# w2 of FFN 1 in five groups: T2 by accumulating transfers, low parts by VectorE, and a new order around the first norms

## The chip, the cores and the metric

The kernel runs on one core of one Trainium2 chip. The metric is the device time of one execution in microseconds (us). Before the change the median of three runs is 1115.6 us (1115.53 to 1117.86).

The engines are named as the profile names them: PE (TensorE) does matrix products, PEld is its weight load, DVE (VectorE) and ACT (ScalarE) work element by element, POOL (GpSimd) and SP (SyncE) here mostly issue transfers. Each engine works through its own list of instructions in order; semaphores hold an instruction until what it needs is there.

## The reference

One layer of a streaming encoder on a batch of one, 512 tokens, width 1024, all in float32:

```python
h = x + 0.5 * post1(SwiGLU_1(pre1(x)))          # D_FF = 2816
u = pre_mix(h)
q, k, v, x_rnn, x_gate = split(u @ w_in)
yA = griffin(x_rnn, x_gate)                      # conv(4), RG-LRU scan, gelu gate
yB = window_attention(q, k, v)
h = h + post_mix((gateA * yA + gateB * yB) @ w_o)
y = h + 0.5 * post2(SwiGLU_2(pre2(h)))
def swiglu(x, w1, w3, w2):
    return (jax.nn.silu(x @ w1) * (x @ w3)) @ w2
```

`pre`, `post` and `pre_mix` are RMS norms with a gain. The change is in the product of the first SwiGLU with its w2 (2816 by 1024), in the norm behind it (post1, then pre_mix), and in the first weights of w_in (the blocks called xr, for x_rnn) which are made ready meanwhile.

## The kernel before

**Three products for one.** TensorE multiplies in a shortened float format (fp32r). To keep float32 accuracy each operand is split into a high part and a low part, and each product is made as hi times hi, plus lo times hi, plus hi times lo. The high part is a copy by ScalarE into the short format (`whi`, L651 for w2, L159/L178 for other weights; `uT`, `hx`, `hT` by L213 for the hidden activations). The low part, `wlo`, comes in one of two ways. Either VectorE subtracts high part from raw value (L659, L179; L214 for activations). Or "by add": ScalarE writes the negated copy (L653, L656, L160), and a transfer issued by POOL adds the raw values onto it while it writes (L654, L657, L161).

**w2 of FFN 1.** The 22 blocks of 128 rows of w2 are worked in two ways. Twenty of them form five groups (`GS_A`, G = 5) of four blocks, each taken as a 2 by 2 block product with seven instead of eight multiplications (class `Halves`, with the Winograd form of Strassen's scheme). The seven are named m1, m5, m2, m6, m3, m7, m4 and are run in that order, five groups each: 35 units, numbered u = 0 to 34, of 12 matmuls with 512 columns (L680 to L682). The weights of a group are b11, b12, b21 and b22. The scheme needs T1 = b12 - b11 for m5 and T2 = b22 - T1 for m2 and for later differences, and similar sums of the activations (`S`, L590). T1 is made by add: ScalarE writes -b11 (L601) and a transfer adds b12 (L602). T2 is a VectorE subtraction (`t2`, L587), for groups 0 to 2 in the units of m5, for 3 and 4 in those of m2. b22 is loaded by SP (L580), and once more for m3 (L665), since it was overwritten.

The remaining two blocks, the tail (`TAIL_A` = 2, 3), are multiplied in the plain way (`classical`, L242 to L244). Their hidden activations are the `kept` blocks (L1318 to L1325).

**Preparing and multiplying.** `step(u)` first prepares unit u + LEAD, LEAD being 5 (`prep`: high part, low part, split of the activations, then the sums), runs hooks that are attached to u, and then issues the unit's matmuls. Bank results are copied out behind the last unit of an m (`out`: L694 on ScalarE, L692 on VectorE for m7). Which units' low parts are made by add stands in the code: m2 of groups 0 to 3, the set `ADD_A` (m6 and m7 of groups 3 and 4, m4 of group 1), and the tail by `BY_DMA`.

**The order around the norms** is written out in `tok_gemm`, in its branch for `pre`: units 0 to 24, the tail products of token tiles 0 and 1, preparation up to unit 31, norm(0); the five units of m7, tail products of tiles 2 and 3, the rest of the preparations, norm(1); then for tiles 2 and 3 in turn half of m4's matmuls, the transposes (L341) of tile t - 2, their copies into `uT` (L351 on ScalarE, L353 on VectorE), and the remaining tail products; norm(2) falls in the first turn. Then the next weights (xr) are split, and norm(3) and the xr products (L224 to L226) follow. A norm starts on VectorE with L294, or L297, and ends with `hg` (L331 on VectorE, L332 on ScalarE), which the transposes need.

**Buffers.** All large tiles share one pool of 42 slots (`NSLOT`). A slot is free again when the last reader of its tile is done; the next tile in program order then takes it. So ScalarE, which writes most new tiles first, can be held by TensorE, which reads the old ones last.

## Time and profile before

| | us |
|---|---|
| median of three runs | 1115.6 |
| profiled execution, its own time | 1117.63 |
| its span | 1115.8 |
| PE busy (98%) | 1097.1 |
| DVE busy (84%) | 934.5 |
| ACT busy (63%) | 698.2 |
| POOL busy (36%) | 404.0 |
| w2 of FFN 1 on PE, first unit to first product of xr | 232.24 to 352.02 |

The mean granted clock of TensorE is 0.993 of full speed. The profiled execution was 2.0 us longer than the median; 1.8 us of its time lie outside the span.

How to read it: busy shares are means over stages with different limits. In the stage of w2 of FFN 1 (about 232 to 352 us) the engines hand work on in a ring: ScalarE and VectorE (or a transfer) make a unit's operands ready, TensorE uses them and frees their slots, and ScalarE needs a free slot for the next one. So the rows to look at are what each engine waited for, and at which time. A row of the timeline has a start, a duration, the engine, the line, the operation, output <- inputs with their shapes; in brackets stand the idle time before it and what ended that.

### The profile page before, as it was taken

What the parts mean: (1) busy time and instruction counts of PE and PEld (TensorE: products, weight loads), DVE (VectorE), ACT (ScalarE), POOL (GpSimd) and SP (SyncE); (2) the same over time, 40 slices, a digit from 0 to 9 for tenths busy, and PEclk for the clock granted to TensorE, in tenths of its full rate; (3) what the DMA queues carried; (4) which work ended last, traced back from release to release, by engine and by line L of the source; (5) the groups of instructions that cost most, each with busy time, mean ns of one, the idle gap of its engine ahead of it and who ended that gap; (6) DMA issues with size and microseconds to landing.
All of it is one profiled execution on the core that took longest, in us unless ns stands there. A gap on an engine that the chain in (4) does not pass through costs nothing.

```text
span 1115.8 us, 18010 instructions
## 1 busy us (share of the span) xinstructions
PE 1097.1 (98%) x6826; PEld 988.5 (89%) x6826; DVE 934.5 (84%) x1329; ACT 698.2 (63%) x1207; POOL 404.0 (36%) x337
## 2 busy tenths in 40 slices
PE   9999999999888999999999999999999999999997
PEld 7899999987677877899888888888999999998886
DVE  5978999999868978878677875867789989999995
ACT  7756555587876677856565665346555555467672
POOL 0144833222111523043555564010777566521000
PEclk9999999999989999999999999999999999999999
DMA  9325653498784572126322345251433233647642
GB/s 333 122 89 131 151 124 114 133 245 196 196 206 135 162 177 99 57 83 247 126 85 87 95 170 208 79 224 58 142 104 114 84 106 96 206 136 186 189 115 92
DMA packets 53926, 159.07 MB, mean 143 GB/s; under 512 B 5568, under 2 KB 7488, under 8 KB 53840
## 3 DMA queue, kind: packets, MB, share of 16 engines
q1 hardware_dynamic: 44640, 132.19, 34.6%
q0 software_dynamic: 8912, 25.21, 11.9%
q8 instruction: 53, 0.87, 0.3%
q10 hardware_dynamic: 288, 0.52, 0.2%
q14 instruction: 33, 0.27, 0.1%
HBM read 137.47 MB, written 13.62 MB: 135 GB/s over the span
## 4 chain that ended last, share of the span: by engine, by line
PE 88%; ACT 4%; issue 3%; DMA 3%; DVE 2%; POOL 0%; DVEq 0%; SPq 0%; POOLq 0%; ACTq 0%
PE c L798 13%; PE c L800 13%; PE c L799 13%; PE f L224 9%; PE f L225 9%; PE f L226 9%; PE hw L681 4%; PE hw L680 3%; PE hw L682 3%; PE acc L242 1%; PE acc L244 1%; PE acc L243 1%; DMA wlo<-raw_w2a 1%; PE pt L1652 1%; DMA wlo<-in_w2a_dram 1%
## 5 line engine op out<-in xcount | busy, mean ns | idle before, releaser
L799 PE MATMUL c<-uT,wlo 128*128 128x256 f32 x516 | 146.0, 283 | 0.0
L800 PE MATMUL c<-uT,whi 128*128 128x256 f32 x516 | 146.0, 283 | 0.0
L798 PE MATMUL c<-uT,whi 128*128 128x256 f32 x516 | 146.0, 283 | 0.0
L798 PE MATMUL c<-Xh,whi 128*128 128x256 f32 x504 | 142.7, 283 | 0.0
L799 PE MATMUL c<-Xh,wlo 128*128 128x256 f32 x504 | 142.6, 283 | 0.0
L224 PE MATMUL f<-uT,whi 128*128 128x512 f32 (+1 forms) x368 | 137.2, 373 | 0.0
L226 PE MATMUL f<-uT,whi 128*128 128x512 f32 (+1 forms) x368 | 135.4, 368 | 0.2 <-DVE uT L353 0.2
L225 PE MATMUL f<-uT,wlo 128*128 128x512 f32 (+1 forms) x368 | 135.3, 368 | 0.0
L800 PE MATMUL c<-Xl,whi 128*128 128x256 f32 x456 | 129.1, 283 | 0.0
L214 DVE TENSOR_TENSOR wlo<-S,whi 128x1024 fp32r<-128x1024 f32 x86 | 121.0, 1407 | 7.3 <-POOL OL L1688 4.5
L213 ACT ACTIVATE whi<-S 128x1024 fp32r<-128x1024 f32 x86 | 88.5, 1055 | 30.2 <-DVE S L847 28.0
L799 PEld LDWEIGHTS c<-uT,wlo 128*128 128x128 f32 x516 | 99.0, 192 | 0.2
L798 PEld LDWEIGHTS c<-uT,whi 128*128 128x128 f32 x516 | 99.0, 192 | 0.2
L800 PEld LDWEIGHTS c<-uT,whi 128*128 128x128 f32 x516 | 99.0, 192 | 0.0
L798 PEld LDWEIGHTS c<-Xh,whi 128*128 128x128 f32 x504 | 96.8, 192 | 0.3 <-issue 0.3
L799 PEld LDWEIGHTS c<-Xh,wlo 128*128 128x128 f32 x504 | 96.8, 192 | 0.0
L681 PE MATMUL hw<-wlo,uT 128*128 128x512 f32 x228 | 89.3, 392 | 1.7 <-DMA wlo<-raw_w2a 1.0
L682 PE MATMUL hw<-whi,uT 128*128 128x512 f32 x228 | 88.9, 390 | 0.0
L680 PE MATMUL hw<-whi,uT 128*128 128x512 f32 x228 | 88.8, 389 | 0.0
L800 PEld LDWEIGHTS c<-Xl,whi 128*128 128x128 f32 x456 | 87.5, 192 | 0.0
L224 PEld LDWEIGHTS f<-uT,whi 128*128 128x128 f32 x368 | 70.1, 190 | 12.9 <-issue 1.7
L226 PEld LDWEIGHTS f<-uT,whi 128*128 128x128 f32 x368 | 69.9, 190 | 11.8 <-DVE uT L353 0.4
(439 smaller groups left out, 3184.5 us busy)
## 6 DMA issues: line engine op xcount, KB each, us to landing
raw_w2b<-in_w2b_dram SPq DMA_DIRECT2D x27, 512.0 KB, 4.5
raw_w2a<-in_w2a_dram SPq DMA_DIRECT2D x22, 512.0 KB, 7.3
raw_w1b<-in_w1b_dram SPq DMA_DIRECT2D x22, 512.0 KB, 4.3
raw_w3b<-in_w3b_dram SPq DMA_DIRECT2D x22, 512.0 KB, 4.4
raw_w3a<-in_w3a_dram SPq DMA_DIRECT2D x21, 512.0 KB, 4.7
raw_w1a<-in_w1a_dram SPq DMA_DIRECT2D x20, 512.0 KB, 4.6
raw_wg<-in_wg_dram SPq DMA_DIRECT2D x16, 512.0 KB, 3.7
h<-in_x_dram SPq DMA_DIRECT2D x8, 512.0 KB, 6.3
```

The costliest lines, as they stand in the source:

```text
L213: act.activation(hi, src, AF.Copy)
L214: dve.tensor_tensor(out=lo, in0=src, in1=f32(hi), op=ALU.subtract)
L224: pe.matmul(ps[:, c0:c1], wh[:, s], h_, start=k == 0 and c0 == 0, stop=False, skip_group_check=True)
L225: pe.matmul(ps[:, c0:c1], wl[:, s], h_, start=False, stop=False, skip_group_check=True)
L226: pe.matmul(ps[:, c0:c1], wh[:, s], l_, start=False, stop=k == KT - 1, skip_group_check=True)
L242: pe.matmul(acc[n], x[:, 0, c], wh[:, s], start=first, stop=False, skip_group_check=skip)
L680: pe.matmul(ps, xs[:, 0, j, c], hi[:, j, :], start=start and j == 0, stop=False, skip_group_check=True)
L681: pe.matmul(ps, xs[:, 0, j, c], lo[:, j, :], start=False, stop=False, skip_group_check=True)
L682: pe.matmul(ps, xs[:, 1, j, c], hi[:, j, :], start=False, stop=i == self.G - 1, skip_group_check=True)
L798: pe.matmul(ps, wh[:, s], xh, start=first, stop=False, skip_group_check=True)
L799: pe.matmul(ps, wl[:, s], xh, start=False, stop=False, skip_group_check=True)
L800: pe.matmul(ps, wh[:, s], xl, start=False, stop=k == 3, skip_group_check=True)
```

## The change

It has four parts.

1. `add_t` takes the place of `add_t1`: for FFN 1, T2 too is made by add, for all five groups. ScalarE writes -T1 into a new slot (the same helper, `T_load`, as for T1), and a transfer issued by POOL adds b22 from HBM. This stands in the units of m5. VectorE's five subtractions for T2 are gone, and so are SP's five first loads of b22.
2. All low parts of w2 of FFN 1 that were made by add are now VectorE subtractions: four of m2, two of m6, two of m7, one of m4, two of the tail; eleven in all. ScalarE's negated copies and POOL's transfers for them are gone.
3. The preparations of m4 of groups 0 and 1 move from ahead of norm(0) to behind it (5G + LEAD + 2 becomes 5G + LEAD). The two gain vectors are loaded five units later, and the scaling of one of them by ScalarE moves from unit 20 to just ahead of norm(0).
4. The splits of the weight blocks xr2 and xr3 move from just ahead of norm(3) to m4's units 31 and 33, which in program order is behind norm(1) and ahead of norm(2).

In total ScalarE has 6 instructions fewer in its list (1038 to 1032), VectorE 6 more (1289 to 1295), POOL 6 fewer (277 to 271), SP 5 fewer (268 to 263). TensorE's order is the same.

ScalarE in the units of m5; `whi` is the high part of T1, `uT<-hEO` a high part of activations. Before:

```order
L651 ACTIVATE whi_2914<-raw_w2a_2739 128x1024
L213 ACTIVATE uT<-hEO_788 128x512
L651 ACTIVATE whi_2936<-raw_w2a_2763 128x1024
L213 ACTIVATE uT<-hEO_1316 128x512
L651 ACTIVATE whi_2958<-raw_w2a_2793 128x1024
```

After:

```order
L659 ACTIVATE whi_2904<-raw_w2a_2739 128x1024
L213 ACTIVATE uT<-hEO_788 128x512
L596 ACTIVATE raw_w2a_2910<-raw_w2a_2739 128x1024
L659 ACTIVATE whi_2928<-raw_w2a_2763 128x1024
L213 ACTIVATE uT<-hEO_1316 128x512
L596 ACTIVATE raw_w2a_2934<-raw_w2a_2763 128x1024
```

Behind each unit's pair now stands a third copy, the negated T1 (L596), onto which the transfer adds b22.

VectorE from the middle of m3's and m7's preparations to the start of norm(0), which is the L294 row; `hT` are the tail's activations. Before:

```order
L214 TENSOR_TENSOR hT_3366<-kept_440,hT_3366 128x512
L659 TENSOR_TENSOR wlo_3387<-raw_w2a_2599,whi_3386 128x1024
L214 TENSOR_TENSOR uT<-hEO_1316,uT 128x512
L214 TENSOR_TENSOR hT_3392<-kept_535,hT_3392 128x512
L659 TENSOR_TENSOR wlo_3415<-raw_w2a_2601,whi_3414 128x1024
L214 TENSOR_TENSOR uT<-hEO_1837,uT 128x512
L214 TENSOR_TENSOR uT<-hEO_2338,uT 128x512
L214 TENSOR_TENSOR uT<-hEO_482,uT 128x512
L659 TENSOR_TENSOR wlo_3487<-raw_w2a_2934,whi_3486 128x1024
L214 TENSOR_TENSOR hx_3488<-hEO_789,hx_3488 128x512
L214 TENSOR_TENSOR hx_3495<-hEO_1317,hx_3495 128x512
L294 TENSOR_TENSOR hc_2999<-hw_3128,hc_2999 128x512
```

After:

```order
L179 TENSOR_TENSOR wlo_3363<-raw_w2a_499_3274,whi_3362 128x1024
L667 TENSOR_TENSOR wlo_3379<-raw_w2a_2599,whi_3378 128x1024
L214 TENSOR_TENSOR uT<-hEO_1316,uT 128x512
L214 TENSOR_TENSOR hT_3384<-kept_535,hT_3384 128x512
L179 TENSOR_TENSOR wlo_3388<-raw_w2a_502_3295,whi_3387 128x1024
L667 TENSOR_TENSOR wlo_3406<-raw_w2a_2601,whi_3405 128x1024
L214 TENSOR_TENSOR uT<-hEO_1837,uT 128x512
L667 TENSOR_TENSOR wlo_3424<-raw_w2a_2717,whi_3423 128x1024
L214 TENSOR_TENSOR uT<-hEO_2338,uT 128x512
L667 TENSOR_TENSOR wlo_3470<-raw_w2a_2719,whi_3469 128x1024
L214 TENSOR_TENSOR uT<-hEO_482,uT 128x512
L294 TENSOR_TENSOR hc_2998<-hw_3120,hc_2998 128x512
```

Four low parts are new ahead of the norm (two L179 of the tail, and `wlo_3424` and `wlo_3470` of m7), and the first units of m4 (`wlo_3487` with the two `hx`) are gone from there.

VectorE from the end of norm(1), whose last row is L331, to the start of norm(2). Before:

```order
L331 SCALAR_TENSOR_TENSOR hg_3656<-h_3400,r_586_3686,bc_mix_pre_g_3126 128x512
L353 TENSOR_TENSOR uT<-tr_3726,uT 128x4x128
L353 TENSOR_TENSOR uT<-tr_3731,uT 128x4x128
L294 TENSOR_TENSOR hc_3112<-acc_3635,hc_3112 128x512
L297 SCALAR_TENSOR_TENSOR fg_3752<-hc_3112,bc_ffn_post_g_3124 128x512
```

After:

```order
L331 SCALAR_TENSOR_TENSOR hg_3645<-h_3391,r_586_3675,bc_mix_pre_g_3231 128x512
L179 TENSOR_TENSOR wlo_3698<-raw_xr_557_3580,whi_3697 128x1024
L179 TENSOR_TENSOR wlo_3714<-raw_xr_564_3608,whi_3713 128x1024
L353 TENSOR_TENSOR uT<-tr_3723,uT 128x4x128
L353 TENSOR_TENSOR uT<-tr_3728,uT 128x4x128
L294 TENSOR_TENSOR hc_3109<-acc_3624,hc_3109 128x512
L297 SCALAR_TENSOR_TENSOR fg_3749<-hc_3109,bc_ffn_post_g_3229 128x512
```

The low parts of xr2 and xr3 (L179) now stand between norm(1) and the copies of the first transposed tile. Where they stood before, from the end of norm(2) to norm(3). Before:

```order
L331 SCALAR_TENSOR_TENSOR hg_3748<-h_3565,r_604_3777,bc_mix_pre_g_3126 128x512
L353 TENSOR_TENSOR uT<-tr_3817,uT 128x4x128
L353 TENSOR_TENSOR uT<-tr_3822,uT 128x4x128
L179 TENSOR_TENSOR wlo_3838<-raw_xr_557_3591,whi_3837 128x1024
L179 TENSOR_TENSOR wlo_3842<-raw_xr_564_3619,whi_3841 128x1024
L294 TENSOR_TENSOR hc_3112<-acc_3642,hc_3112 128x512
```

After:

```order
L331 SCALAR_TENSOR_TENSOR hg_3745<-h_3554,r_608_3774,bc_mix_pre_g_3231 128x512
L353 TENSOR_TENSOR uT<-tr_3814,uT 128x4x128
L353 TENSOR_TENSOR uT<-tr_3819,uT 128x4x128
L294 TENSOR_TENSOR hc_3109<-acc_3631,hc_3109 128x512
L297 SCALAR_TENSOR_TENSOR fg_3877<-hc_3109,bc_ffn_post_g_3229 128x512
```

Norm(3) now follows the transposed tile directly.

The diff:

```diff
@@ -419,8 +419,7 @@
 
         if pre:
             G = pre.G
-            pre.hooks[2 * G].append(vectors)
-            pre.hooks[4 * G].append(lambda: act.activation(g[1], g[1], AF.Copy, scale=NEWT))
+            pre.hooks[3 * G].append(vectors)
             for i in range(2):
                 pre.hooks[6 * G - 2 + i].append(lambda i=i: [split_to(st["get"] + i + 1), dma_to(st["get"] + i + 3)])
             for u in range(5 * G):
@@ -430,7 +429,8 @@
                 acc[t] = [pre.bank["bc"][t], pre.bank["bx"][t]]
                 for n_ in range(2):
                     classical(t, n_)
-            pre.prep(5 * G + LEAD + 2)
+            pre.prep(5 * G + LEAD)
+            act.activation(g[1], g[1], AF.Copy, scale=NEWT)
             norm(0)
             for u in range(5 * G, 6 * G):
                 pre.step(u)
@@ -438,10 +438,13 @@
                 acc[t] = [pre.bank["bu"][t - 2], bank("acc")]
                 classical(t, 1)
             pre.prep(7 * G)
+            pre.hid.eo.clear()
             norm(1)
             for t in range(2, 4):
                 for u in range(6 * G, 7 * G):
                     pre.step(u, (t - 2,))
+                    if t == 2 and u % G % 2:
+                        split_to(st["split"] + 1)
                 trs[t - 2] = transpose_mm(us[t - 2])
                 transpose_out(trs[t - 2], t - 2, xf if t == 2 else None)
                 classical(t, 0)
@@ -449,7 +452,6 @@
                     norm(2)
             split_to(st["get"] + len(first))
             dma_to(st["split"] + 2)
-            pre.hid.eo.clear()
             pre.bank.clear()
         else:
             tails()
@@ -555,14 +557,14 @@
 
         names = ("m1", "m5", "m2", "m6", "m3", "m7", "m4")
 
-        def __init__(self, nm, hid, hooks, gs, by_add, in_slots, add_t1):
+        def __init__(self, nm, hid, hooks, gs, by_add, in_slots, add_t):
             self.nm, self.hid, self.hooks, self.gs = nm, hid, hooks, gs
             self.by_add, self.in_slots = by_add, in_slots
             self.G = G = len(gs)
-            self.loads = [(b, i) for i in range(G) for b in (("b11",) if add_t1 else ("b11", "b12"))]
+            self.loads = [(b, i) for i in range(G) for b in (("b11",) if add_t else ("b11", "b12"))]
             self.first = len(self.loads)
-            self.loads += [(b, i) for b in ("b22", "b21") for i in range(G)]
-            self.add_t1 = add_t1
+            self.loads += [(b, i) for b in (("b21",) if add_t else ("b22", "b21")) for i in range(G)]
+            self.add_t = add_t
             self.again_at = self.names.index("m3") * G - 3
             self.raw, self.ops, self.loaded, self.ready = {}, {}, 0, 0
             self.bank, self.c, self.again, self.did = {}, {}, {}, set()
@@ -589,17 +591,23 @@
         def S(self, o, p, q, i, op=ALU.subtract):
             dve.tensor_tensor(out=self.x(i, *o), in0=self.x(i, *p), in1=self.x(i, *q), op=op)
 
+        def T_load(self, o, q, i):
+            t = self.raw[o, i] = slot([P, 2, 512], name=f"raw_{self.nm}")
+            act.activation(t, self.raw[q, i], AF.Copy, scale=-1.0)
+            pool.dma_start(out=t, in_=self.src(o, i), accum_op=ALU.add)
+
         def t2(self, i):
-            self.T("b22", "b22", "b12", i)
+            if self.add_t:
+                self.T_load("b22", "b12", i)
+            else:
+                self.T("b22", "b22", "b12", i)
             del self.raw["b12", i]
 
         def t1(self, i):
             if ("t", i) not in self.did:
                 self.did.add(("t", i))
-                if self.add_t1:
-                    t = self.raw["b12", i] = slot([P, 2, 512], name=f"raw_{self.nm}")
-                    act.activation(t, self.raw["b11", i], AF.Copy, scale=-1.0)
-                    pool.dma_start(out=t, in_=self.src("b12", i), accum_op=ALU.add)
+                if self.add_t:
+                    self.T_load("b12", "b11", i)
                 else:
                     self.T("b12", "b12", "b11", i)
 
@@ -614,11 +622,11 @@
                 self.t1(i)
                 self.s1(i)
             elif m == "m5":
-                if i < T2_EARLY:
+                if i < T2_EARLY or self.add_t:
                     self.t2(i)
                 self.S((0, 0), (0, 1), (0, 0), i)
             elif m == "m2":
-                if i >= T2_EARLY:
+                if i >= T2_EARLY and not self.add_t:
                     self.t2(i)
                 self.T("b11", "b22", "b11", i)
                 self.S((1, 0), (1, 0), (0, 0), i)
@@ -639,7 +647,7 @@
                 self.ready += 1
                 m, i = self.names[u // G], u % G
                 if load:
-                    self.load(min(self.first + 2 * G, self.first + (u if u >= U_SLOTS else u == 3)))
+                    self.load(self.first + (max(0, u - G) if self.add_t else u if u >= U_SLOTS else u == 3))
                 b, odd, half = self.OPERANDS[m]
                 hi = slot([P, 2, 512], F32R, name="whi")
                 lo = slot([P, 2, 512], F32R, name="wlo")
@@ -649,7 +657,7 @@
                     xs = uT[:, :, (u + 1) % 8, :].rearrange("p e (j c) -> p e j c", j=2)
                 src = self.again.pop(i) if m == "m3" else self.raw[b, i]
                 act.activation(hi, src, AF.Copy)
-                if m == "m2" and i < 4:
+                if m == "m2" and i < 4 and not self.add_t:
                     act.activation(lo, src, AF.Copy, scale=-1.0)
                     pool.dma_start(out=lo, in_=self.src(b, i), accum_op=ALU.add)
                 elif (m, i) in self.by_add:
@@ -708,7 +716,7 @@
                 later(0, lambda: self.out(m), 0)
             point()
 
-    def blocks(nm, hid, pairs, late, h_src, gs, marks, by_add, in_slots, loads, add_t1=False):
+    def blocks(nm, hid, pairs, late, h_src, gs, marks, by_add, in_slots, loads, add_t=False):
 
         hooks = {u: [] for u in range(7 * len(gs))}
 
@@ -723,7 +731,7 @@
         for at_, fn in zip(marks, (lambda n: dma_to(st["get"] + n + 1), tail_tile, h_back)):
             for n, u in enumerate(at_):
                 hooks[u].append(lambda n=n, fn=fn: fn(n))
-        half = Halves(nm, hid, hooks, gs, by_add, in_slots, add_t1)
+        half = Halves(nm, hid, hooks, gs, by_add, in_slots, add_t)
         pairs.more = lambda n: half.load(loads[n])
         ahead = lambda: half.prep(min(half.ready + 1, U_SLOTS))
         end = len(pairs.jobs) - 1
@@ -1808,7 +1816,7 @@
 GRAW_AT = (29, 30)
 TB_AT = (34, 35, 36, 37)
 
-BY_DMA = {("wg", i) for i in range(2)} | {("w2a", i) for i in (2, 3)} | {("xr", i) for i in range(2)}
+BY_DMA = {("wg", i) for i in range(2)} | {("xr", i) for i in range(2)}
 
 BY_POOL = {("wg", i) for i in range(2, 8)} | {("wk", 0), ("wk", 1)}
 
@@ -1819,7 +1827,7 @@
 LOAD_A, LOAD_B = (0, 3, 5, 5), (0, 6, 8, 10)
 GS_A = (4, 6), (8, 10), (12, 14), (16, 18), (0, 20)
 MARKS_A = (17, 18), (21, 22), (20, 22, 27, 29)
-ADD_A = {(m, i) for m in ("m6", "m7") for i in (3, 4)} | {("m4", 1)}
+ADD_A = set()
 
 TAIL_B = (20, 21)
 GS_B = (0, 2), (4, 6), (8, 10), (12, 14), (16, 18)
```

## The prediction

> **What bounds the kernel now.** I read first how busy the engines are over the whole span, then the busy time by stretches around w2 of FFN 1, then TensorE's waits there, and last VectorE's own rows.
>
> ```profile
> PE 1097.1 (98%) x6826; PEld 988.5 (89%) x6826; DVE 934.5 (84%) x1329; ACT 698.2 (63%) x1207; POOL 404.0 (36%) x337
> ```
>
> ```profile
> 364.25:1100.00 735.75, 735.75 (x4512) 660.16 (x4511) 616.32 (x881) 450.08 (x805) 302.46 (x235) 1.00 0.41 132
> 232.24:295.85 63.61, 61.87 (x270) 49.75 (x269) 63.51 (x80) 48.21 (x65) 10.11 (x10) 1.00 0.90 240
> 309.12:315.95 6.83, 5.98 (x14) 4.73 (x15) 3.11 (x4) 4.02 (x6) 1.51 (x2) 0.50 0.99 232
> 363.72:367.14 3.42, 3.42 (x18) 3.42 (x17) 1.95 (x3) 3.11 (x7) 0.36 (x1) 0.50 1.00 382
> ```
>
> The columns are the stretch, its length, then busy time of PE, PEld, DVE, ACT, POOL, then granted clock, DMA share and GB/s. From 364.25 to 1100 TensorE is never idle and the change touches nothing there, so what it gains or loses by 364 reaches the end one for one. In the w2 stage VectorE is full instead (63.51 of 63.61 us), and TensorE runs into waits:
>
> ```profile
> PE hw L243 <- DMA wlo<-in_w2a_dram: 5.3, 2, 4.0
> PE tr L341 <- DVE hg L331: 3.4, 1, 3.4
> PE hw L681 <- DMA wlo<-raw_w2a: 1.0, 1, 1.0
> PE hw L681 <- DMA wlo<-in_w2a_dram: 0.8, 3, 0.3
> ```
>
> Columns: total, times, longest. The tail blocks' low parts by DMA cost 5.3 us and, behind the 4.0 us wait, the clock of 0.50 for 6.83 us, in which 5.98 us of busy time do the work of 3.0. Yet that is not what sets the end. TensorE waits once more, 3.4 us for `hg` of the fourth norm, norm(3), and that is the end of a VectorE chain:
>
> ```profile
> 239.19 1.22 DVE L659 TENSOR_TENSOR wlo<-raw_w2a,whi 128x1024 fp32r<-128x1024 f32 x1
> 240.32 0.68 DVE L214 TENSOR_TENSOR uT<-hEO,uT 128x512 fp32r<-128x512 f32 x1
> 240.93 1.21 DVE L587 TENSOR_TENSOR raw_w2a<-raw_w2a,raw_w2a 128x1024 f32<-128x1024 f32 x1
> 254.90 1.21 DVE L587 TENSOR_TENSOR raw_w2a<-raw_w2a,raw_w2a 128x1024 f32<-128x1024 f32 x1
> 284.75 0.68 DVE L1318 TENSOR_TENSOR kept<-kept,Rb 128x512 f32<-128x512 f32 x1
> 315.97 0.68 DVE L294 TENSOR_TENSOR hc<-hw,hc 128x512 f32<-128x512 f32 x1
> 324.32 0.75 DVE L331 SCALAR_TENSOR_TENSOR hg<-h,r,bc_mix_pre_g 128x512 f32<-128x512 f32 x1
> 326.09 1.23 DVE L659 TENSOR_TENSOR wlo<-raw_w2a,whi 128x1024 fp32r<-128x1024 f32 x1 [1.01 <-ACT whi L651]
> 334.57 0.68 DVE L294 TENSOR_TENSOR hc<-hw,hc 128x512 f32<-128x512 f32 x1
> 341.69 0.75 DVE L331 SCALAR_TENSOR_TENSOR hg<-h,r,bc_mix_pre_g 128x512 f32<-128x512 f32 x1
> 342.94 1.29 DVE L353 TENSOR_TENSOR uT<-tr,uT 128x512 fp32r<-128x512 f32 x2 [0.49 <-ACT uT L351]
> 344.14 0.68 DVE L294 TENSOR_TENSOR hc<-acc,hc 128x512 f32<-128x512 f32 x1
> 352.00 1.29 DVE L353 TENSOR_TENSOR uT<-tr,uT 128x512 fp32r<-128x512 f32 x2 [0.49 <-ACT uT L351]
> 353.44 1.23 DVE L179 TENSOR_TENSOR wlo<-raw_xr,whi 128x1024 fp32r<-128x1024 f32 x1
> 355.71 0.68 DVE L294 TENSOR_TENSOR hc<-acc,hc 128x512 f32<-128x512 f32 x1
> ```
>
> Columns: start, duration, engine, line. L294 starts a norm (315.97, 334.57, 344.14, 355.71). Start to start, a 1024-wide subtraction takes 1.13 us (239.19 to 240.32) and a 512-wide one 0.61 (240.32 to 240.93). I use these pitches, not the longer durations, because neighbours overlap.
>
> TensorE's own rows at the end of the stage:
>
> ```profile
> 352.02 0.39 PE L224 MATMUL f<-uT,whi 128*128 128x256 f32 x1
> 359.35 0.28 PE L225 MATMUL f<-uT,wlo 128*128 128x256 f32 x1
> 359.47 0.28 PE L226 MATMUL f<-uT,whi 128*128 128x256 f32 x1
> 363.14 1.45 PE L341 MATMUL tr<-ident,hg 128*128 128x128 f32 x8 [3.39 <-DVE hg L331]
> ```
>
> The first xr products start at 352.02, as soon as the second token tile is transposed, and are over at about 359.6.
>
> **The change, along VectorE's chain.**
>
> *To the end of m6.* Five T2 subtractions (L587) go, four low parts of m2 and two of m6 come: 6 - 5 = +1 times 1.13 = +1.1 us. For T2 ScalarE now writes a negated copy, and its rows give the price:
>
> ```profile
> 236.83 1.04 ACT L601 ACTIVATE raw_w2a<-raw_w2a 128x1024 f32<-128x1024 f32 x1
> 237.78 1.04 ACT L651 ACTIVATE whi<-raw_w2a 128x1024 fp32r<-128x1024 f32 x1
> 238.73 0.62 ACT L213 ACTIVATE uT<-hEO 128x512 fp32r<-128x512 f32 x1
> 239.25 1.05 ACT L651 ACTIVATE whi<-raw_w2a 128x1024 fp32r<-128x1024 f32 x1
> ```
>
> A wide copy takes 0.95 us, a narrow one 0.52. A unit of m5 costs ScalarE 0.95 + 0.95 + 0.52 = 2.42 us and VectorE 1.13 + 2 x 0.61 = 2.35, so for five units ScalarE is the slower by 0.4; two evacuations of m1 (L692) add up to 1.0 on ScalarE. VectorE thus waits 0 to 1.4 us; I take 1.1. m6 ends at 284.75 + 1.1 + 1.1 = 287.0.
>
> T2's transfer itself, bounded from both sides:
>
> ```profile
> raw_w2a<-in_w2a_dram POOLq DMA_DIRECT2D x5, 512.0 KB, 9.4
> DMA to landing us min/median/max: 3.6/7.3/13.9
> ```
>
> The same kind (T1) takes 9.4 us in the middle; the shortest raw transfer of w2 3.6, the longest 13.9. T2 of group 0 starts when ScalarE has written its copy, at about 240.2 in m5. VectorE first reads it in m2, at 254.90 now, less three T2 subtractions, plus one low part: 252.6, plus up to 1.4 of waits. So 3.6 and 9.4 cost nothing and 13.9 up to 1.5 us; I take nothing, by T1's row, and the later groups have more time, since a unit of m2 is longer than one of m5.
>
> Eleven other accumulating transfers and five plain loads go from a stretch with DMA at 0.90, so later transfers should not get slower; the loads of b21 on SP stay at their units. POOL loses six instructions and its two broadcasts move five units later, far ahead of the norm that reads them. The scaling of the gain, one wide copy on ScalarE, moves to just ahead of the first norm: 0 if ScalarE is idle there, 0.95 if not. I take 0, since VectorE is the later one there, with its two tail low parts.
>
> *From m6 to the first norm.* VectorE does four narrow instructions for the kept blocks (L1318 and its like), ten units of m3 and m7 with 1.13 + 0.61 each, two narrow for the tail's hidden blocks and two wide low parts for the tail: 2.4 + 17.4 + 1.2 + 2.3 = 23.3 us. The two m4 units are now behind the norm. In the trace this stretch holds long waits:
>
> ```profile
> DVE hx L214 <- ACT hx L213: 3.4, 1, 3.4
> DVE wlo L659 <- ACT whi L651: 3.1, 3, 2.2
> DVE uT L214 <- ACT uT L213: 3.1, 2, 1.9
> ```
>
> That is 9.6 us between 295 and 316, and I let all of it go: ScalarE was held by TensorE, which held the weight slots while it waited for the tail's DMA, and that wait ends with the DMA. The tail's second low part is now ready at about 305, 1.7 us after TensorE wants it, in place of 5.3. The first norm starts at 287.0 + 23.3 = 310.3, 5.7 us ahead of 315.97. TensorE's tail products are done by about 309.7, in time.
>
> *First to second norm.* The norm holds VectorE for 9.0 us (315.97 to about 325.0): 319.3. Then come all five m4 units, 5 x 1.74 = 8.7, two evacuations of m7 (1.2), and waits of the kind seen at 326.09 (1.01 for ScalarE, which also splits two xr blocks there): 2.6 in sum, from one such wait for each of two or three units. The second norm starts at 331.85 against 334.57: half the lead is spent on m4.
>
> *Second to third norm.* `hg` comes 7.12 us after the norm's start (334.57 to 341.69), at 339.0. New here: low parts of xr2 and xr3, 2.3 us, and about 1.1 us of waiting for ScalarE's high parts. With the transposed tile behind it the third norm starts at 344.2, against 344.14: the lead is gone.
>
> *Third to fourth norm.* Now it comes back: the xr low parts that stood at 353.44 are already done, so the fourth norm starts when the uT rows at 352.00 end, at 353.3 and not at 355.71. Its transposes can start 363.14 - 355.71 = 7.43 later, at 360.7 against 363.14: a gain of 2.4 us.
>
> *TensorE beside it.* Of 10.1 us (5.3 + 1.0 + 0.8 of waits and 3.0 of half clock) it gets back 1.7 at the tail and, by my sums of VectorE's lateness, 0.5 each in m6 and m4, and comes to the end of the m4 products at 352.0 - 10.1 + 2.7 = 344.6. There it has nothing: the xr products need the tile of 352.00. It idles 7.4 us, which is new. The trace shows what such a gap does: 0.50 of the clock from 309.12 after the 4.0 us, and from 363.72 after 3.39 us, both lifted in steps of 3.42 us. From 352.0 there are about 50 matmuls at 0.12 us (359.35 to 359.47) and 0.9 for a transposition, 7.0 us at full clock. Half clock for one to two steps (3.4 to 6.8 us) loses 1.7 to 3.4: ready between 360.7 and 362.4; on the steps of this trace (363.72 less two is 356.9, where it lifts), 361.45. It takes VectorE's place as the last by 0.75 us. Behind it there is no more idle time, so the 0.50 from 363.72 to 367.14, which loses 1.7, goes too.
>
> The Trainium skill ("TensorE: Matmul & The Clock Gate", section "Part 1: The HAM clock gate (the "warmup" mystery)") says that the clock is halved after an idle window of about 3.4 us and that the windows run free of the kernel. That speaks against this change, which makes the longest gap of the stage; the trace agrees (0.50 after 4.0 and 3.39 us idle), and a window that falls badly gives the later of the two ends above.
>
> **The sum** against the profiled run, 1117.63 us with a span of 1115.8: 361.45 - 363.14 = -1.7, and -1.7 for the clock: -3.4, so 1114.2. The median is 1115.6, 2.0 us below that run. Such a run may well lack the 1.7 of the second half clock, since a gap of 3.39 us hardly fills a step of 3.42; against it the gain would be 1.7 and the time 1113.9. If the 2.0 us are something else, 3.4 and 1112.2. Nothing shown tells which, so I take the middle, 2.5: **1113.1 us**.
>
> **The rivals.**
> *More gain.* The waits that I added (1.1 + 2.6 + 1.1 = 4.8 us) stay away. Then the tile of 352.0 comes at 347.2, TensorE's gap is 2.7 us, too short for the half clock, and it is ready at 354.2; the norm sets 355.9. Gain 7.2: 1108.4; with half of the waits about 1110.5. For it: ScalarE has 15 us free in the 63.6. Against: each of the waits has a row like it.
>
> *No difference.* Of the 9.6 us that I remove, 2 to 5 stay, since a unit of m3 asks for ScalarE and VectorE in turn. Each us delays all three later norms; 0.75 is free, the rest counts: 1113.1 + 2 - 0.75 = 1114.3 up to 1117.4.
>
> *Slower.* The ring of three closes in m3 and m7:
>
> ```profile
> L651 ACT ACTIVATE whi<-raw_w2a 128x1024 fp32r<-128x1024 f32 x26 | 27.3, 1052 | 12.9 <-PE hw L681 6.3 <-DMA raw_w2a<-in_w2a_dram 4.4 <-PE hw L682 2.2
> ```
>
> Between 239 and 316 ScalarE's high parts waited 8.5 us for slots that TensorE held. If TensorE, late in m6 and m3 because VectorE now makes every low part, holds them again, VectorE keeps waits as before. My margin is about 3 us of TensorE's lateness. With all 9.6 us the first norm starts at 319.9, 4 us after 315.97, and the end is at 1113.1 + 9.6 - 0.75 = 1122.0. It crosses the bound with 5.5 us.
>
> *The change doesn't do what it says* has no room: the new order on every engine shows each step.
>
> **The numbers.** 0.2% is 2.2 us, about what a measurement can tell: faster means below 1113.4, slower above 1117.8. The forecast has 0.42, its own range 1111.5 to 1114.2, 0.30 of it below 1113.4; more gain 0.18; no difference 0.18; slower 0.22. So faster 0.48, same 0.30, slower 0.22. The range goes from 1109.5 (most of the waits absent) to 1118.5 (6.2 of the 9.6 us kept).
>
> **What would show it.** Right: no wait of TensorE for a DMA of w2; norms starting near 310, 332, 344 and 353; a new gap of TensorE near 344 to 352 with half clock behind it; no gap at the fourth norm's transposes. Wrong: VectorE waiting for ScalarE by more than 3 us before the first norm; TensorE waiting for T2's DMA in m2; the third norm after 346, which hands every further us to the end; or the gap at 352 closed, which would mean that the chain is shorter than I summed.

## The result, and the profile after

The changed kernel takes 1114.18 us (median of 14 runs, 1113.33 to 1115.43). In the same comparison the kernel before takes 1117.26 us (median of 14 runs, 1115.53 to 1120.01). The ratio is 0.9973, with a 95% interval of 0.9965 to 0.9981: 3.1 us, or 0.27%, faster. The profiled execution of the changed kernel took 1113.81 us with a span of 1112.0, against 1117.63 and 1115.8 before.

Note the kernel before: its median was 1115.6 over the three runs that the prediction saw, and is 1117.26 over fourteen. Its profiled execution was close to the middle, and the median of three was at the low end.

The profile page of the changed kernel, engines' busy time:

```profile
PE 1094.1 (98%) x6826; PEld 986.9 (89%) x6826; DVE 940.6 (85%) x1335; ACT 692.1 (62%) x1201; POOL 398.6 (36%) x331
```

VectorE has 6.1 us more to do than before, and the kernel is faster. So the gain cannot be read from the busy shares; it is in the waits. TensorE's waits from 232 to 365 us (total, times, longest):

```profile
PE f L224 <- ACT uT L351: 4.4, 1, 4.4
PE hw L688 <- DVE hc L700: 2.9, 1, 2.9
PE hw L243 <- DVE wlo L179: 1.3, 1, 1.3
PE hw L689 <- DVE wlo L667: 0.7, 1, 0.7
```

No wait for a DMA is left. The 5.3 us for the tail's transfers have become 1.3 us for VectorE's low part, and the 3.4 us ahead of the fourth norm's transposes are gone. Two waits are new: 2.9 us at the start of m4, and 4.4 us for the second transposed tile. VectorE's waits from 295 to 316, where there were 9.6 us before:

```profile
DVE e L263 <- ACT r L259: 1.4, 1, 1.4
```

That one lies within norm(0), and the kernel before has it too. VectorE's timeline, at the places the prediction named (L1326 is the end of m6, L294 starts a norm, L331 ends one):

```profile
286.86 0.68 DVE L1326 TENSOR_TENSOR kept<-kept,Rb 128x512 f32<-128x512 f32 x1
310.12 0.69 DVE L294 TENSOR_TENSOR hc<-hw,hc 128x512 f32<-128x512 f32 x1
331.63 0.68 DVE L294 TENSOR_TENSOR hc<-hw,hc 128x512 f32<-128x512 f32 x1
340.47 2.36 DVE L179 TENSOR_TENSOR wlo<-raw_xr,whi 128x1024 fp32r<-128x1024 f32 x2 [0.95 <-ACT whi L178]
343.95 0.68 DVE L294 TENSOR_TENSOR hc<-acc,hc 128x512 f32<-128x512 f32 x1
353.08 0.68 DVE L294 TENSOR_TENSOR hc<-acc,hc 128x512 f32<-128x512 f32 x1
359.70 0.75 DVE L331 SCALAR_TENSOR_TENSOR hg<-h,r,bc_mix_pre_g 128x512 f32<-128x512 f32 x1
```

And TensorE's timeline, its idle times at m4's start and at the second tile, and its transposes of the fourth norm, which follow a product without a gap:

```profile
329.10 0.47 PE L688 MATMUL hw<-whi,hx 128*128 128x512 f32 x1 [2.90 <-DVE hc L700]
351.89 0.58 PE L224 MATMUL f<-uT,whi 128*128 128x256 f32 x1 [4.42 <-ACT uT L351]
360.47 0.28 PE L226 MATMUL f<-uT,whi 128*128 128x256 f32 x1
360.59 0.60 PE L341 MATMUL tr<-ident,hg 128*128 128x128 f32 x4
```

The clock by stretches (columns as in the prediction):

```profile
351.90:355.47 3.57, 3.57 (x17) 3.35 (x18) 3.11 (x6) 2.07 (x7) 0.00 (x0) 0.55 0.68 243
355.47:360.59 5.12, 5.12 (x45) 5.12 (x44) 4.63 (x13) 3.99 (x10) 0.00 (x0) 1.00 0.41 126
364.00:1100.00 736.00, 736.00 (x4509) 659.70 (x4508) 617.15 (x884) 448.77 (x803) 301.82 (x235) 1.00 0.41 130
```

After the gap of 4.42 us the clock is half until about 355.1, one step of 3.41 us (the first row holds a little of full clock too, so its mean is 0.55). Since TensorE had time there, this costs nothing that VectorE does not cost anyway. From 364 on TensorE is full, as before. The fourth transposes come 363.14 - 360.59 = 2.55 us earlier, and the half clock from 363.72 to 367.14, which lost 1.7, is gone: 4.25 us in sum. TensorE's last matmul starts 4.18 us earlier (1104.62 instead of 1108.80). The span fell by 3.8, since in these two executions the time behind the last matmul was some 0.4 us longer after the change.

### The profile page after: what moved, and what is told of

Read it like the earlier page. It is cut to its first block, busy times and chain, and to the rows that moved or that the text cites. A ratio compares the mean times of both kernels' runs of the same rounds, so it can differ in the third digit from the quotient of the medians.

```text
span 1112.0 us, 17985 instructions
## 1 busy us (share of the span) xinstructions
PE 1094.1 (98%) x6826; PEld 986.9 (89%) x6826; DVE 940.6 (85%) x1335; ACT 692.1 (62%) x1201; POOL 398.6 (36%) x331
## 4 chain that ended last, share of the span: by engine, by line
PE 94%; DVE 2%; ACT 2%; issue 1%; DMA 0%; DVEq 0%; SPq 0%; ACTq 0%
PE c L806 13%; PE c L807 13%; PE c L808 13%; PE f L224 10%; PE f L226 9%; PE f L225 9%; PE hw L690 5%; PE hw L688 5%; PE hw L689 5%; PE acc L243 1%; PE acc L242 1%; PE acc L244 1%; PE pt L1660 1%; DVE wlo L667 1%; PE s L1624 1%
```

## The experiments

The theory: from m5 to the fourth norm one chain of VectorE's work, with what it waits for, sets the time at which the fourth norm's transposes can start; TensorE behind it is always full. Every instruction taken from VectorE, and every wait, counts as long as TensorE or ScalarE is not later. The main rival: the gain is simply TensorE's 5.3 us of waiting for the tail's transfers with the half clock behind it. All ratios are to the kernel before, run on the same chip.

### Undoing part 4: the splits of xr2 and xr3

```diff
                     pre.step(u, (t - 2,))
-                    if t == 2 and u % G % 2:
-                        split_to(st["split"] + 1)
```

> The changed kernel with part 4 undone: the splits of xr2 and xr3 stand again just ahead of norm(3). Theory (VectorE's chain through the four norms sets the time): norm(2) starts 3.3 us earlier (2.3 of low parts and 1.0 of waiting gone from ahead of it), at 340.6 instead of 343.95; the transposed tile is ready at 348.5 instead of 351.9, so TensorE's gap of 4.4 us at 347.5 shrinks to about 1; norm(3) then starts behind the two low parts at 352.0 instead of 353.1, its transposes at 359.5 instead of 360.6, and TensorE waits for them some 4 us, with half clock behind that costing 1.7. In sum -1.1 + 1.7: 1114.8 us, within 1 of the changed kernel's 1114.2. Rival (part 4 alone is what brings the gain at the fourth norm, as my sum had it: 2.3 us come back): 1116.5.

Measured: 1114.5 us (1113.2 to 1114.91), ratio 0.9977 (0.9969 to 0.9986). TensorE's wait, the stretch behind it (clock third from the end), and VectorE's start of norm(3):

```profile
359.91 1.97 PE L341 MATMUL tr<-ident,hg 128*128 128x128 f32 x8 [3.39 <-DVE hg L331]
359.90:367.00 7.10, 7.09 (x49) 7.10 (x50) 4.09 (x5) 6.09 (x10) 2.86 (x2) 0.79 1.00 381
352.48 0.68 DVE L294 TENSOR_TENSOR hc<-acc,hc 128x512 f32<-128x512 f32 x1
```

Norm(3) starts 0.6 us earlier without part 4 (352.48 against 353.08), since VectorE no longer waits 0.95 us for ScalarE there. But TensorE gets the second tile early, runs out, waits 3.39 us, and runs at 0.79 of the clock on average from 359.9 to 367.0. The two effects cancel. Part 4 alone brings nothing that can be measured; it puts TensorE's idle time where it costs less.

### Undoing part 1: T2 by transfer

```diff
         def t2(self, i):
-            if self.add_t:
-                self.T_load("b22", "b12", i)
-            else:
-                self.T("b22", "b22", "b12", i)
+            self.T("b22", "b22", "b12", i)
...
-            self.loads += [(b, i) for b in (("b21",) if add_t else ("b22", "b21")) for i in range(G)]
+            self.loads += [(b, i) for b in ("b22", "b21") for i in range(G)]
...
-                if i < T2_EARLY or self.add_t:
+                if i < T2_EARLY:
...
-                if i >= T2_EARLY and not self.add_t:
+                if i >= T2_EARLY:
```

> The changed kernel with part 1 undone: T2 by VectorE again, b22 loaded by SP. Theory (VectorE's chain): five subtractions of 1.13 us come back, 5.7, less about 1.1 us that VectorE waits for ScalarE in m5: norm(0) starts at 314.6 instead of 310.1, everything behind it as much later, the last transposes at 365.1 instead of 360.6: 1118.7 us. Rival (the gain is TensorE's 5.3 us of waiting for the tail's transfers and the half clock behind it, and VectorE has room): 1114.2, as the changed kernel.

Measured: 1118.76 us (1118.07 to 1120.1), ratio 1.0019 (1.0010 to 1.0027). VectorE's first norm:

```profile
314.94 0.69 DVE L294 TENSOR_TENSOR hc<-hw,hc 128x512 f32<-128x512 f32 x1
```

The theory came out within 0.1 us in the time and 0.4 us in the place. The rival is out: TensorE has no wait for the tail's transfers in this kernel, and yet it is slower than the kernel before. VectorE had no room.

### One edit alone on the kernel before: the tail's low parts

```diff
-BY_DMA = {("wg", i) for i in range(2)} | {("w2a", i) for i in (2, 3)} | {("xr", i) for i in range(2)}
+BY_DMA = {("wg", i) for i in range(2)} | {("xr", i) for i in range(2)}
```

> The kernel before with one edit: the low parts of the two tail blocks by VectorE instead of by transfer. Theory (VectorE's chain, whose 9.6 us of waiting between 295 and 316 come from the tail's transfers by way of TensorE and ScalarE): VectorE gets 2.3 us of work and loses most of the 9.6: norm(0) at 309 to 313 instead of 316, the last transposes at 356 to 360 instead of 363.1, 1109 to 1114 us, so as good as the whole change or better. Rival (the other parts are needed, because VectorE, with T2 still on it, takes the wait over): norm(0) at 316 to 318, 1115.6 to 1118.

Measured: 1113.51 us (1111.05 to 1114.53), ratio 0.9967 (0.9955 to 0.9979). That is as good as the whole change. TensorE's two long waits from 300 to 365:

```profile
PE hw L680 <- DVE hc L692: 3.6, 1, 3.6
PE tr L341 <- DVE hg L331: 3.4, 1, 3.4
```

VectorE's norms start at 311.49, 330.05, 339.62 and 351.19: with 2.3 us more to do, norm(0) is 4.5 us earlier. From 295 to norm(0) VectorE now waits 3.4 us where it waited 9.6. So most of that waiting did come from the tail's transfers; that the way is by TensorE and ScalarE's slots fits the rows, where ScalarE waits for TensorE, but it was not varied alone. All the rest of the change together adds nothing to this one line.

### Undoing part 3: the first two units of m4 ahead of norm(0)

```diff
-            pre.hooks[3 * G].append(vectors)
+            pre.hooks[2 * G].append(vectors)
+            pre.hooks[4 * G].append(lambda: act.activation(g[1], g[1], AF.Copy, scale=NEWT))
...
-            pre.prep(5 * G + LEAD)
-            act.activation(g[1], g[1], AF.Copy, scale=NEWT)
+            pre.prep(5 * G + LEAD + 2)
```

> The changed kernel with part 3 undone: the first two units of m4 are prepared ahead of norm(0) again, the gain vectors loaded and scaled at their old units. Theory (VectorE's chain counts every instruction once, wherever it stands ahead of norm(1)): norm(0) starts 3.5 us later, at 313.6, norm(1) and all behind it where they are, at 331.6: 1114.2 us, within 0.5. Rival (the preparations ahead of norm(0) must wait for slots that TensorE still holds, as the hx wait of 3.4 us before shows): norm(0) at 316 or later, norm(1) at 334: 1116.5.

Measured: 1114.57 us (1113.76 to 1116.77), ratio 0.9980 (0.9971 to 0.9988), no difference from the changed kernel that can be told. The norms start at 313.07, 331.71, 344.01 and 353.14: the first 3 us later, the others within 0.1 us. Here moving work within the chain changes nothing behind it.

### Undoing part 2: all eleven low parts by transfer

```diff
-                if m == "m2" and i < 4 and not self.add_t:
+                if m == "m2" and i < 4:
...
-BY_DMA = {("wg", i) for i in range(2)} | {("xr", i) for i in range(2)}
+BY_DMA = {("wg", i) for i in range(2)} | {("w2a", i) for i in (2, 3)} | {("xr", i) for i in range(2)}
...
-ADD_A = set()
+ADD_A = {(m, i) for m in ("m6", "m7") for i in (3, 4)} | {("m4", 1)}
```

> The changed kernel with part 2 undone: all eleven low parts by transfer again. Theory (the tail's transfers stop TensorE, by it ScalarE's slots, and by them VectorE): VectorE has 11.3 us less to do ahead of norm(0) but waits for most of it; TensorE waits again some 5 us for the tail's transfers, and norm(0) starts at 312 to 315 instead of 310.1: 1116 to 1118 us. Rival (VectorE's work alone sets the chain, and transfers are free): norm(0) at 300 to 305, 1109 or less.

Measured: 1120.11 us (1119.25 to 1124.3), ratio 1.0030 (1.0019 to 1.0041), slower than either theory had it. VectorE has much less to do and waits for all of it. Its waits from 232 to 365, the three largest, and TensorE's:

```profile
DVE wlo L667 <- ACT whi L659: 9.6, 11, 1.9
DVE uT L214 <- ACT uT L213: 6.6, 5, 1.9
DVE wlo L667 <- ACT kept L1329: 2.2, 1, 2.2
```

```profile
PE hw L689 <- DMA wlo<-in_w2a_dram: 6.0, 1, 6.0
PE f L224 <- ACT uT L351: 3.9, 1, 3.9
PE hw L243 <- DMA wlo<-in_w2a_dram: 3.7, 2, 2.2
```

The 6.0 us stand in m2, ahead of 265.81, and neither theory had named them. So there are two waits for transfers here, and the next run takes them apart.

### Only m2's four low parts by transfer

```diff
-                if m == "m2" and i < 4 and not self.add_t:
+                if m == "m2" and i < 4:
```

> The changed kernel with four of its eleven low parts, those of m2, by transfer again. Theory (part 1 and part 2 depend on each other: with T2's transfers on GpSimd's queue, which land one per 2.5 us, the transfers for m2 come behind them and land late): TensorE waits about 6 us for the first of them in m2, as with all eleven by transfer, although VectorE has 4.5 us less to do; norm(0) at 311 to 314 instead of 310.1: 1115 to 1118 us. Rival (the 5.9 us lost with all eleven by transfer came from the tail's transfers alone): no wait in m2, norm(0) at 306 to 308, 1110 to 1112.

Measured: 1118.15 us (1116.31 to 1119.12), ratio 1.0005 (0.9996 to 1.0013). TensorE in m2, and the DMA issues of GpSimd's queue from 232 to 262 (KB each, median us from issue to landing):

```profile
265.78 0.79 PE L689 MATMUL hw<-wlo,uT 128*128 128x512 f32 x1 [6.04 <-DMA wlo<-in_w2a_dram]
```

```profile
raw_w2a<-in_w2a_dram POOLq DMA_DIRECT2D x7, 512.0 KB, 12.0
wlo<-in_w2a_dram POOLq DMA_DIRECT2D x4, 512.0 KB, 12.9
```

The same window in the kernel before:

```profile
wlo<-in_w2a_dram POOLq DMA_DIRECT2D x4, 512.0 KB, 7.9
```

So the low parts of m2 took 7.9 us on this queue, and 12.9 with T2's transfers ahead of them. Norm(0) starts at 313.89, as expected, and the time is 0.15 us above the expected range. So parts 1 and 2 hang together: T2 by transfer takes the place on GpSimd's queue that m2's low parts had, and these must go to VectorE. T2 frees VectorE of 5 subtractions, m2 gives it 4 back. What is left of both is one subtraction.

### Only m6, m7 and m4's five low parts by transfer

```diff
-ADD_A = set()
+ADD_A = {(m, i) for m in ("m6", "m7") for i in (3, 4)} | {("m4", 1)}
```

> The changed kernel with five of the eleven low parts (m6 and m7 of groups 3 and 4, m4 of group 1) by transfer again, m2 and the tail by VectorE. Theory (VectorE's chain, and these transfers have time to land): VectorE has 4.5 us less to do ahead of norm(0), which starts at 306 to 309 instead of 310.1, held by TensorE's tail products at the earlier end; the last transposes 1 to 3 us earlier: 1111 to 1113 us. Rival (each low part by transfer costs ScalarE's time and makes TensorE wait, as 1.0 us in the kernel before): norm(0) at 310 or later, 1114 to 1116.

Measured: 1111.41 us (1111.26 to 1112.18), ratio 0.9949 (0.9937 to 0.9960), so 2.8 us better than the whole change; the intervals do not touch. Norm(0) starts at 305.95 and norm(3) at 349.93. TensorE does not wait for these five transfers here (in the kernel before it had waited 1.0 us for one of them, at 287.07). Giving them to VectorE was a loss inside the change. Of the 4.5 us taken from VectorE ahead of norm(0) and the 1.1 behind it, norm(0) shows 4.2 and norm(3) 3.2.

### The xr low parts by transfer

```diff
-BY_DMA = {("wg", i) for i in range(2)} | {("xr", i) for i in range(2)}
+BY_DMA = {("wg", i) for i in range(2)} | {("xr", i) for i in range(4)}
```

> The changed kernel with the low parts of xr2 and xr3 made by transfer (as those of xr0 and xr1 are), so that VectorE has neither between norm(1) and norm(2). Theory (VectorE's chain): norm(2) at 340.6 instead of 343.95, the transposed tile at 348.5 instead of 351.9, norm(3) at 349.8 instead of 353.1, its transposes at 357.2 instead of 360.6; no half clock at 352: 1110.8 us. Rival (TensorE is the last there, and what VectorE gains is lost in its next wait or in a wait for the transfers): 1113.5 to 1114.5.

Measured: 1114.89 us (1114.49 to 1116.03), ratio 0.9983 (0.9974 to 0.9992): no gain; the theory missed by 4 us. ScalarE's timeline between norm(1) and the copy of the transposed tile:

```profile
339.36 1.04 ACT L159 ACTIVATE whi<-raw_xr 128x1024 fp32r<-128x1024 f32 x1
340.31 1.04 ACT L160 ACTIVATE wlo<-raw_xr 128x1024 fp32r<-128x1024 f32 x1
341.25 1.04 ACT L159 ACTIVATE whi<-raw_xr 128x1024 fp32r<-128x1024 f32 x1
342.20 1.04 ACT L160 ACTIVATE wlo<-raw_xr 128x1024 fp32r<-128x1024 f32 x1
343.15 1.06 ACT L351 ACTIVATE uT<-tr 128x512 fp32r<-128x512 f32 x2
```

A low part by transfer costs ScalarE a second copy. The copy of the tile, which VectorE needs, comes at 343.15 instead of 341.29, and VectorE waits up to 4.3 us for it. My expectation had priced VectorE only. The chain at this place belongs to ScalarE as much as to VectorE.

### The xr splits by GpSimd, at part 4's place

```diff
+LO_POOL = {("xr", 2), ("xr", 3)}
-BY_POOL = {("wg", i) for i in range(2, 8)} | {("wk", 0), ("wk", 1)}
+BY_POOL = {("wg", i) for i in range(2, 8)} | {("wk", 0), ("wk", 1)} | LO_POOL
...
-                dve.tensor_tensor(out=lo, in0=r, in1=f32(hi), op=ALU.subtract)
+                (pool if order[k] in LO_POOL else dve).tensor_tensor(out=lo, in0=r, in1=f32(hi), op=ALU.subtract)
```

> The changed kernel with both parts of xr2 and xr3 made by GpSimd, which is idle there, so that neither ScalarE nor VectorE does them. The run with their low parts by transfer lost time because ScalarE's two more copies (0.95 us each) stood ahead of its copy of the transposed tile. Theory (the chain VectorE and ScalarE share between the norms): norm(2) at 340.6 instead of 343.95, the tile at 349.5, norm(3) at 350.0 instead of 353.1, its transposes at 357.5 instead of 360.6, TensorE's gap at 347.5 down to 2 us and no half clock: 1111 us. Rival (GpSimd's copies and subtractions, by its rows 1.2 and 3.0 us each, come too late for the third xr unit, or slow VectorE down): 1113.5 to 1116.

Measured: 1114.78 us (1114.46 to 1116.4), ratio 0.9978 (0.9969 to 0.9986): no gain again. GpSimd's rows, and VectorE's beside them in norm(1):

```profile
332.58 2.71 POOL L179 TENSOR_TENSOR wlo<-raw_xr,whi 128x1024 fp32r<-128x1024 f32 x1
336.82 2.81 POOL L179 TENSOR_TENSOR wlo<-raw_xr,whi 128x1024 fp32r<-128x1024 f32 x1
```

```profile
333.18 0.68 DVE L294 TENSOR_TENSOR hc<-hw,hc 128x512 f32<-128x512 f32 x1
333.89 1.95 DVE L297 SCALAR_TENSOR_TENSOR fg<-hc,bc_ffn_post_g 128x512 f32<-128x512 f32 x1
336.64 3.54 DVE L308 SCALAR_TENSOR_TENSOR h<-fg,r,h 128x512 f32<-128x512 f32 x2
```

The same instructions in the changed kernel:

```profile
334.02 0.69 DVE L297 SCALAR_TENSOR_TENSOR fg<-hc,bc_ffn_post_g 128x512 f32<-128x512 f32 x1
335.66 1.42 DVE L308 SCALAR_TENSOR_TENSOR h<-fg,r,h 128x512 f32<-128x512 f32 x2
```

L297 takes 1.95 us instead of 0.69 and the pair L308 3.54 instead of 1.42, while GpSimd subtracts. L294, which reads one of its inputs from TensorE's banks, keeps its 0.68. From norm(1)'s start to its `hg` VectorE needs 10.35 us instead of 7.14, and these 3.2 us are all that the move had freed (2.3 of low parts and 0.95 of waiting).

### The same on the kernel before with the tail's edit

The edits are those of the tail alone and of the run above, on the kernel before.

> The kernel before with two edits: the tail's low parts by VectorE, and xr2 and xr3 by GpSimd. Theory: with the tail alone norm(3) starts at 351.2, of which 2.3 to 4.5 us are the xr low parts and VectorE's wait for ScalarE's high parts; without them norm(3) at 347 to 349, its transposes at 354.5 to 356.5 instead of 358.5, a gap of at most 1.5 us there and so no half clock behind it (1.7): 1113.5 less 3.7 to 5.7, 1108 to 1110 us. Rival (as in the run before this): 1113 or more.

Measured: 1109.45 us (1108.94 to 1112.05), ratio 0.9933 (0.9920 to 0.9945). Here GpSimd's work falls beside norm(2), which takes 7.27 us to its `hg` instead of 6.62: 0.65 lost, not 3.2. Norm(3) starts at 348.89, the gap at its transposes is 0.89 us, and no half clock follows.

### GpSimd's splits in the changed kernel, without part 4

The edits are those that undo part 4 and those of the GpSimd run.

> The changed kernel with part 4 undone and xr2 and xr3 made by GpSimd. In the run where GpSimd did this at part 4's place, VectorE's instructions in norm(1) took up to twice as long beside it (L308 3.54 us instead of 1.42), which ate the gain. Theory (VectorE is slowed only while GpSimd subtracts beside it; in this order the work falls mostly beside norm(2) and costs some 0.7 us there, as with the tail alone): norm(2) at 341 to 342, norm(3) at 350 to 351.5 instead of 352.5, transposes at 358, a gap below 2 us and no half clock: 1110 to 1111.5 us. Rival (the slowing costs 3 us wherever the work falls): 1113 to 1115.

Measured: 1112.28 us (1111.48 to 1112.97), ratio 0.9955 (0.9943 to 0.9967). Norm(2) at 341.00, norm(3) at 350.71, as the theory had it; the time is 0.8 us above its range, 1.9 us better than the changed kernel (all five runs are below its fastest, though the two intervals of the ratio just overlap). Where GpSimd's work falls decides what it costs VectorE.

### Both improvements together

The edits are those of the run above and the five low parts by transfer.

> Both edits together: part 4 undone, xr2 and xr3 by GpSimd, the five low parts of m6, m7 and m4 by transfer. Theory: the two gains add, since both shorten VectorE's chain, until TensorE itself is the last: 1107 to 1109.5 us, as good as or better than the kernel before with only the tail and xr edits (1109.45). Rival (T2 by transfer and its third copy on ScalarE in m5 are what costs): 1110 to 1112.

Measured: 1109.21 us (1108.86 to 1109.81), ratio 0.9928 (0.9916 to 0.9940), the fastest of all, though not to be told from the kernel before with tail and xr edits alone. TensorE's waits in it from 300 to 365, down to 0.9 us:

```profile
PE hw L686 <- DVE hc L698: 2.4, 1, 2.4
PE hw L243 <- DVE wlo L179: 1.2, 1, 1.2
PE tr L341 <- DVE hg L331: 0.9, 1, 0.9
PE f L224 <- ACT uT L351: 0.9, 1, 0.9
```

The two gains, 2.8 and 1.9 us, give 5.0 together. This kernel and the one before with tail and xr edits differ by part 1, m2's low parts and part 3. So these three together bring nothing there that can be told (1109.21 against 1109.45), and the rival, that T2 by transfer is what costs, is out as well.

### What each piece is worth

| piece, against the changed kernel's 1114.18 | us without it | worth in the change |
|---|---|---|
| part 1, T2 by transfer | 1118.76 | 4.6 gained |
| part 2, m2's low parts by VectorE | 1118.15 | 4.0 gained, given part 1 |
| part 2, m6, m7 and m4's low parts by VectorE | 1111.41 | 2.8 lost |
| part 2, the tail's low parts by VectorE | not run alone | on the kernel before: 3.7 gained |
| part 3, the order at norm(0) | 1114.57 | none to be told |
| part 4, the place of the xr splits | 1114.5 | none to be told |

The runs stand in several comparisons, each with its own runs of the kernel before; taken by the ratios the worths differ by up to 0.5 us. The pieces do not add up, because part 1 and m2's low parts each repair what the other breaks.

## Why the prediction was right

The sign, and the mechanism, were right, and the places more exactly than the sum:

| step | predicted | measured |
|---|---|---|
| end of m6 | 287.0 | 286.86 |
| first norm | 310.3 | 310.12 |
| second norm | 331.85 | 331.63 |
| third norm | 344.2 | 343.95 |
| fourth norm | 353.3 | 353.08 |
| the last transposes | 361.45 (norm: 360.7) | 360.59 |
| TensorE's wait for the tail | 1.7 | 1.3 |
| TensorE's idle time from m7 to the second tile | one gap of 7.4 | 2.90 + 4.42 |

Point by point:

- **VectorE as the pacer.** Right. Putting T2 back on it alone costs 4.6 us, close to its five subtractions (5.65 us) less the 0.86 us for which VectorE waits for ScalarE in m5 when T2 is made by transfer. The waits for ScalarE that the sum took as 1.1, 2.6 and 1.1 us measure 0.86, 2.3 (0.95, 1.00 and 0.34) and 0.95.
- **All of the 9.6 us goes.** Right, and for the reason given: the tail's edit alone frees most of it.
- **T2's transfer costs nothing.** Right for VectorE, which never waits for it. But the sentence that later transfers should not get slower was wrong: T1's and T2's transfers take 12.0 us in the middle where the same queue showed 9.9 before in the same window. There was time for it in m5; there was none for m2's low parts behind them, as the run that puts them there shows.
- **TensorE beside it.** The step failed in its form. I had m4's products run on from the tail's to 344.6. They wait 2.9 us at 326.2, because m4's first product needs m7's bank (L700) copied out, and that stands on VectorE behind four units of m4. The idle time of 7.3 us was the same, but in two parts. What followed the second, half clock for one step of 3.41 us, was at the short end of the one to two steps that I allowed, so TensorE was not 0.75 us behind VectorE, but level.
- **"Now it comes back"**, the gain at the fourth norm from the xr splits' new place. Right as an item of the sum, wrong as a cause: with the splits in their old place the fourth norm starts even earlier.
- **The sum.** 3.4 us against the profiled execution, measured 3.1 between the medians and 3.8 between the two profiled executions. Against the median I took 2.5, halfway to 1.7, because I supposed that the three runs lacked a half clock which the profiled one had. With more runs the median moved to the profiled one. The mis-sized term is that discount of 0.9 us; the 1114.2 that the sum gave against the profiled execution is the measured median. That it fits to 0.02 us is luck: TensorE's last transposes came 0.86 us earlier than the sum had them, and some 0.4 us behind the last matmul and 0.4 us between the profiled execution (1113.81) and the median took it back.
- **The rivals.** The ring of TensorE, ScalarE and VectorE did not close in this kernel. It does with m2's low parts by transfer, where VectorE waits 8.6 us for ScalarE again and the kernel is no faster than before. Between 239 and 316 ScalarE's high parts there waited 17.7 us for slots that TensorE held; in the changed kernel it was 7.9, close to the 8.5 before, but VectorE was the later one there and waited only 0.86 us for a high part ahead of norm(0).
- **"Too short for the half clock"**, said of a gap of 2.7 us in the first rival. Wrong as a rule: half clock stands behind nine gaps of 2.40 to 2.92 us in the other runs (last section). The rival did not come true for another reason: the waits that it left out were there.

The Trainium skill ("TensorE: Matmul & The Clock Gate", section "Part 1: The HAM clock gate (the "warmup" mystery)") has the clock fall after an idle window of about 3.4 us. The trace agrees for the gap of 4.42 us and for those of 3.39 us, and behind the gap of 2.90 us at 329.10 the clock stays at 1.00. But half clock also follows gaps of 2.40 us, so the measurement says that less is enough, as the last section works out.

## What to carry to other kernels

When one engine paces a stage, write its chain as a list of starts and add or remove instructions by their start-to-start pitch; the four norms came out within 0.3 us this way. Then do the same for the engine that feeds it, since work taken from the pacer by a transfer may land on the feeder in front of what the pacer needs next. And try a bundle piece by piece: here one line gave the whole gain, two pieces only repaired each other, one lost 2.8 us, and the best versions lie 5 us below the bundle.

## What the runs showed of the hardware that I had not expected

- **GpSimd beside VectorE.** Where GpSimd subtracts two tiles, VectorE's instructions with both tiles in on-chip memory take up to 2.8 times as long (1.95 against 0.69 us), while one with an input in TensorE's banks keeps its time. The rows look like holding, not slowing: L297 ends at 335.84 and the pair L308 at 340.18, each 0.55 us after GpSimd's subtraction beside it (335.29 and 339.63). The Trainium skill ("SBUF — State Buffer", section "Who interferes with whom") says that a VectorE instruction with two inputs in that memory contends with a GpSimd instruction that reads it, and one with at most one such input does not, outside modes that use two ports; the rows agree.
- **A queue of adding transfers.** Seven of 512 KB in a row on GpSimd's queue took 12.0 us each in the middle, and four more behind them 12.9. Over the whole stretch from 232 to 296 the load of DMA fell from 0.90 to 0.77. But in the window where these transfers run it was full before (first row) and after (second row), at 0.99 and 1.11 as the profile counts it, while the GB/s in the last column fell:

```profile
239.00:262.00 23.00, 23.00 (x102) 18.88 (x102) 23.00 (x30) 18.64 (x26) 5.20 (x5) 1.00 0.99 260
239.00:262.00 23.00, 23.00 (x103) 19.04 (x102) 22.14 (x28) 20.73 (x30) 6.59 (x6) 1.00 1.11 245
```

So whether the queue itself or the full DMA engines set the 12 us, no run shows.

- **What halves the clock.** In these traces the clock changes only in steps of 3.41 us, on a grid whose place differs from execution to execution. What sorts the cases is not the length of a gap but how long TensorE is idle within one step. A gap of 2.90 us stands near 329 in the changed kernel (first two rows) and in the one with GpSimd's splits without part 4 (last two rows):

```profile
327.79:331.20 3.41, 2.10 (x9) 1.79 (x10) 3.07 (x5) 2.59 (x4) 0.86 (x1) 1.00 1.04 155
331.20:334.62 3.42, 3.42 (x16) 2.83 (x16) 3.23 (x6) 1.33 (x4) 0.00 (x0) 1.00 0.80 140
326.69:330.10 3.41, 1.21 (x5) 1.05 (x6) 3.08 (x5) 3.41 (x5) 0.86 (x1) 1.00 0.96 163
330.10:333.51 3.41, 3.41 (x9) 2.63 (x8) 3.25 (x6) 0.79 (x3) 0.00 (x0) 0.50 1.03 166
```

In the first the gap is split: 1.59 us fall in the step up to 327.79 and 1.31 in the next, and the clock stays full. In the second 2.20 us fall in one step, and the next step has half clock. Over all fourteen traces, from 20 to 1095 us, 22 steps at full clock hold 1.0 to 1.83 us of idle time, and full clock follows each; 24 hold 1.91 us or more, and half clock follows each. The largest of the first kind is 347.58 to 350.99 in the run without part 3, the smallest of the second 327.07 to 330.48 in the run with GpSimd's splits at part 4's place. No run varied a gap alone, so this is read from the traces and not tested.

- **The spread of runs.** The kernel before spreads over 4.5 us in 14 runs, the changed kernel over 2.1. The length of the longest gap does not sort the kernels: with 3.89 us (xr low parts by transfer) eleven runs spread over 1.5 us, with 2.92 us (T2 on VectorE) eleven over 2.0. That a gap falls on the grid in another place in each execution may be part of it; with one trace of each kernel this stays open.
